# A seven-product down projection whose first and last two steps become eight plain products

## The chip, the cores and the metric

One Trainium2 chip, one NeuronCore. The metric is the device time of one execution in microseconds (us), lower is better. Engines: TensorE (PE in the profile; its weight loads are PEld), VectorE (DVE), ScalarE (ACT), GpSimd (POOL), and SyncE (SP), which here only issues transfers.

## The reference

One inference step of a two-layer trunk: a retention layer, a gated linear attention layer, and behind each a feed-forward network with a causal convolution of width 3. 1024 prompt frames and 32 frames of a running stream (T = 1056 columns), model width 1024, inner width 2816, all float32. The change touches the last feed-forward network's second matrix and the final norm behind it:

```python
def conv_ffn(h, conv_state, w_up, conv_w, conv_b, w_down):
    u = h @ w_up
    ...
    gate, val = jnp.split(c, 2, axis=-1)
    return (jax.nn.silu(gate) * val) @ w_down, ext[:, T:]
...
        y, cs = conv_ffn(h, conv_states[i], ffn_w_up[i], ffn_conv_w[i], ffn_conv_b[i], ffn_w_down[i])
        x = x + y
    return rmsnorm(x, norm_final), ...
```

## The kernel before

**Exactness.** A float32 matrix product is made of three matmuls in the format fp32r: both operands are split into a rounded part ("hi", a cast on ScalarE) and the rest ("lo", a subtraction on VectorE), and hi·hi, hi·lo and lo·hi are added in PSUM.

**Up projection of the last layer** (`ffn_up`, line 1829). 22 tile pairs f of inner width, each by a Winograd form of Strassen's seven products for two halves s of the columns (528 each; the half is cut once more into two quarters of TH = 264, the "b" of the block form). VectorE and ScalarE run the convolution, SiLU and the multiplication (`conv`, line 1858). `pair_sums` (line 1877) then forms, for each pair k of inner tiles (f = 2k, 2k+1; NP = 11 pairs), the seven column combinations that the down projection wants, and stores them to the scratch tensor `scr_h7`, in the order ORD = (1, 2, 6, 5, 7, 4, 3). Pieces 1, 2 and 3 are plain blocks (even tile's first quarter, odd tile's first and second); the others are sums. `ahead_split` (line 1913) splits the pieces of k = 0 and 1, one in each f from 5 to 18, into hi and lo, and stores them to `scr_h2`.

**Down projection** (`Down7`, line 1600). The output has eight tiles of 128 rows, in four pairs p. Step n (0 to 13) handles output pair p = (n+1) mod 4 with a window of at most four K pairs, n-3 to n, cut to 0 to 10; so K pair k is used in steps k to k+3, once for each output pair, and the windows hold 1, 2, 3, then eight times 4, then 3, 2, 1 pairs. For each step, product i of seven and half s, `product` (line 1676) issues three matmuls of 128x264 for each K pair of the window (lines 1689, 1691, 1692). Each half has three PSUM banks a, b and c, where products 1, 6, 7 share a, 2 and 4 share b, 5 and 3 share c; a product that starts a bank anew waits until its previous content is read, and 3, which adds to bank c, waits until line 1707 has read 5 there.

Steps 0 to 9 gather an output block of two quarters in SBUF (`block`: a ring of five blocks for tile 0 of the pair, of three for tile 1), with three ScalarE copies and four VectorE additions for each half (lines 1699 to 1712), and add it to the residual in DRAM by an accumulating transfer (`add`, line 1715, GpSimd's queue); the block returns to its ring when the transfer has landed. Steps 10 to 13 add straight into the residual in SBUF (`settle`, line 1723, after `fetch` has loaded it), square it and, for the last pair, take the final norm and store (`squares`, line 1743; `rms_row` with the matmul of line 231). From step 11 on, the whole of half 0 comes first, then that of half 1.

**What feeds a step.** `weights(k)` (line 1636) asks for a step's two raw matrices (a ring of three raw buffers), splits the first (L1654, L1655), forms sums and differences (L1660 to L1667), and splits those: five casts or copies on ScalarE, eight operations on VectorE, into seven of ten weight buffers. From step 3 on the request stands on GpSimd's queue. `load_x` (line 1618) loads pieces of K pair k on SP's queue; four K pairs live in 28 slots of seven each (slot 7·(k mod 4)+i), so that a piece of pair k+1 goes where that of pair k-3 has just been used. K pairs 0 and 1 come split from `scr_h2`; those from 2 on come raw, and the returned `split` (L1630 on ScalarE, L1633 on VectorE) splits them in place. For k > 3, one is loaded after each product pair of the step before (SP waits for that product), and its split is taken from the list `late` once more than three are there.

**What sets the order.** The kernel is written in program order, but a planner of the framework places each engine's instructions by its own estimate of when they are ready, the place in the program being a priority; `order(a, b)` only forces a behind b. Each engine then works strictly in the placed order, and waits by semaphores. `run` (line 1787) holds the places: weights at i = 0 or 2 of the step before, the last convolution at step 2, `early` (line 1771) the first loads inside the last f of the up projection.

Of the kernel before, what the change touches and what calls it, by code (L numbers as in the profile page):

```python
# [9 lines left out]
F32 = mybir.dt.float32  # L10
# [40 lines left out]
def trunk_kernel(ctx: ExitStack, tc: tile.TileContext, io):  # L51
# [1546 lines left out]
    NP = NF // 2  # L1598

    class Down7:  # L1600

        def __init__(self, sm, regions, AR, HR):
# [3 lines left out]
            self.Y, self.splits, self.ends = {}, [], {}  # L1606
# [11 lines left out]
        def load_x(self, k, i, n=1):  # L1618
            reg, j = self.at[7 * (k % 4) + i]
            v = reg[:, j * 4 * TH:(j + n) * 4 * TH].rearrange("p (m j u) -> p m j u", m=n, j=2)  # L1620
            for m in range(n):
                self.X[k, ORD[i + m]] = v[:, m].rearrange("p j (s t) -> p j s t", s=2)
# [13 lines left out]
        def weights(self, n, home=None, queue=nc.sync):  # L1636
            h = len(self.win[n]) * P
            a, b = slice(0, h), slice(h, 2 * h)
            rg, rv = raw_tile(f"dg{uid()}"), raw_tile(f"dv{uid()}")
            for j, r in enumerate((rg, rv)):  # L1640
                o = self.offs[n] + j * 2 * h * P
                queue.dma_start(r[:, :2 * h], io["w_down7"][o:o + 2 * h * P].rearrange("(p c) -> p c", p=P))

            at = [0]

            def tile(name):
                if home is None:
                    return w_tile(f"{name}{uid()}")
                at[0] += 2 * h
                return home[:, at[0] - 2 * h:at[0]]  # L1650

            def split(src, name):
                hi, lo = tile(name + "h"), tile(name + "l")
                S.copy(hi[:, :2 * h], src[:, :2 * h])  # L1654
                V.tensor_tensor(lo[:, :2 * h], src[:, :2 * h], hi[:, :2 * h].bitcast(F32), op=ALU.subtract)  # L1655
                return [(hi[:, c], lo[:, c]) for c in (a, b)]

            w = self.W[n] = {}
# [4 lines left out]
            v = tile("dwv")  # L1663
# [11 lines left out]

        def product(self, n, s, i):
            m, win = ORD[i], self.win[n]
# [7 lines left out]
            wh, wl = self.W[n][m]  # L1685
            for j, k in enumerate(win):
                c = slice(j * P, j * P + P)
                x = self.X[k, m][:, :, s]
                PE.matmul(ps, wh[:, c], x[:, 0], start=m in (1, 2, 4, 5) and j == 0, stop=False,  # L1689
                          skip_group_check=True)  # L1690
                PE.matmul(ps, wh[:, c], x[:, 1], start=False, stop=False, skip_group_check=True)  # L1691
                mm = PE.matmul(ps, wl[:, c], x[:, 0], start=False, stop=j == len(win) - 1, skip_group_check=True)  # L1692
            self.ends[n, s, i] = mm
# [77 lines left out]
        def early(self, s, i):  # L1771
            if s == 0 and i:
                if i < 4:
                    self.load_x(0, 2 * i - 2, 2)
                elif i == 4:
                    self.load_x(0, 6)
                    self.load_x(1, 0)
                else:
                    self.load_x(1, 2 * i - 9, 2)
                if i == 2:  # L1780
                    self.weights(0)
            if (s, i) == (1, 4):
                self.load_x(1, 5, 2)
            if (s, i) == (1, 5):
                self.weights(1)

        def run(self, last_conv):
# [3 lines left out]
            late, todo = [], []  # L1791
            for n, s, i in seq:
                self.product(n, s, i)
                k = n + 1
                if s == 0:
                    if n < NP - 2 and k > 1 and i == (2 if n > 2 else 0):
                        self.weights(k, None, G if n > 1 else nc.sync)
                    if n == NP - 2 and i == 2:
                        self.weights(k, None, G)
                        self.fetch(3)  # L1800
                    if n == NP - 1 and i in (1, 4):
                        self.weights(NP if i == 1 else NP + 2, None if i == 1 else self.at[21][0][:, 20 * TH:], G)
                    if n == NP - 1 and i in (1, 3, 5):
                        self.fetch(i // 2)
                    if n == NP and i == 0:
                        self.weights(NP + 1, self.at[24][0], G)
                    continue
                if n >= NP:
                    continue
                if n == 2 and i == 1:  # L1810
                    todo = last_conv()
                if todo and n > 2 and i in (2, 5):
                    todo.pop(0)()
                if k in (2, 3):
                    if i == 0:
                        j = 0
                        while j < 7:
                            at = 7 * (k % 4) + j
                            c = 2 if j < 6 and self.at[at][0] is self.at[at + 1][0] else 1
                            self.splits.append(self.load_x(k, j, c))  # L1820
                            j += c
                    elif i > 2:
                        later(self.splits, 2)
                elif 3 < k < NP:
                    late.append(self.load_x(k, i))
                if len(late) > 3 or late and k >= NP:
                    late.pop(0)(self.ends[n, s, i])

    def ffn_up(l, X, fc, sm, he=None, ready=None):
# [47 lines left out]
        def pair_sums(f, c):  # L1877
# [5 lines left out]
            def keep(m, a):  # L1883
                nc.sync.dma_start(io["scr_h7"][k, :, ORD.index(m)], a)
# [8 lines left out]
            if f % 2 == 0:  # L1893
                keep(1, e[:, 0])
                return
# [430 lines left out]
```

## Time and profile before

| | us |
|---|---|
| median of three runs | 2806.88 (2804.42 to 2809.35) |
| profiled execution | 2807.33 |
| its span, first to last instruction | 2805.6 |
| its mean granted clock | 0.996 |
| first matmul of the down projection (L1689), from the span's start | 2542.6 |
| last norm matmul (L231) | 2791.3 |

A row of a list of instructions reads: start, duration, engine, line, operation, output <- inputs, count, and in brackets the idle time before it with what ended it. `pu` is a PSUM bank, `dw..h` and `dw..l` are split weights, `dg` and `dv` the raw ones, XA, XB and XH hold X, AR and HR the blocks and residual. A row of the waits reads: who waited, for whom, us in total, times, the longest. Recorded matmuls overlap: the distance of two starts, not the duration, is the cost of one in a stream.

### The profile page before, as it was taken

To read this page: it belongs to the slowest core of one execution; us is meant where nothing else is said; L and a number is where in the kernel's file an instruction comes from. 1 tells how busy PE (TensorE), PEld (TensorE's weight loads), DVE (VectorE), ACT (ScalarE), POOL (GpSimd) and SP (SyncE) were. 2 spreads that over 40 slices of the span, in tenths; PEclk is the share of its full clock that TensorE was granted. 3 is DMA by queue.
4 is the path that set the end of the run, shared out by engine and by line. 5 is a ranking of instruction groups with operands and counts; after the bars stand their busy time and mean duration, and the time that the engine had idled before them with its cause. 6 is when DMAs were issued, how large, how long until landed. Compare 5 with 4: busy or idle time off the path is not lost.

```text
span 2805.6 us, 54515 instructions
## 1 busy us (share of the span) xinstructions
PE 2757.1 (98%) x21954; PEld 2666.6 (95%) x21954; DVE 1990.9 (71%) x3456; ACT 1353.8 (48%) x2481; POOL 363.3 (13%) x650
## 2 busy tenths in 40 slices
PE   9999999999999999999999999999999999999997
PEld 9999988888999999999999999999999999999996
DVE  7876666676557877777555576775479888888667
ACT  7544354444435444444444466653355444445444
POOL 0000000000112111111000042220132111112222
PEclk9999999999999999999999999999999999999998
DMA  6333455554875222222855501115533434339882
GB/s 239 94 113 100 146 150 150 139 153 121 281 241 183 82 80 82 75 86 73 269 189 163 177 30 53 53 46 200 190 119 100 150 123 154 113 100 292 208 226 91
DMA packets 238974, 395.04 MB, mean 141 GB/s; under 512 B 59008, under 2 KB 162816, under 8 KB 234112
## 3 DMA queue, kind: packets, MB, share of 16 engines
q1 hardware_dynamic: 222960, 333.51, 36.6%
q0 software_dynamic: 15216, 57.50, 7.5%
q8 instruction: 172, 2.82, 0.4%
q14 instruction: 82, 0.67, 0.1%
q10 hardware_dynamic: 544, 0.54, 0.1%
HBM read 272.25 MB, written 119.23 MB: 140 GB/s over the span
## 4 chain that ended last, share of the span: by engine, by line
PE 81%; DVE 7%; ACT 3%; issue 3%; POOL 3%; DMA 2%; SPq 0%; DVEq 0%; POOLq 0%; ACTq 0%
PE pu L441 13%; PE pu L436 13%; PE pu L440 13%; PE pd L1519 5%; PE pd L1521 5%; PE pd L1520 5%; PE psv L270 2%; PE psv L271 2%; PE psv L272 2%; POOL x L1122 2%; PE pu L1689 2%; PE pu L1691 1%; PE pu L1692 1%; PE pg L133 1%; PE pg L134 1%
## 5 line engine op out<-in xcount | busy, mean ns | idle before, releaser
L110 DVE TENSOR_TENSOR wlo<-raw,whi 128x1024 fp32r<-128x1024 f32 x131 | 163.1, 1249 | 126.9 <-ACT whi L110 119.1
L415 ACT COPY HR<-pu 128x264 f32<-128x264 f32 x264 | 98.6, 374 | 264.6 <-PE pu L441 258.6
L110 ACT CAST whi<-raw 128x1024 fp32r<-128x1024 f32 x131 | 136.9, 1049 | 175.5 <-PE pd L1520 111.3
L441 PE MATMUL pu<-XA,wgl 128*128 128x264 f32 x752 | 213.4, 284 | 0.0
L436 PE MATMUL pu<-XA,wgh 128*128 128x264 f32 x752 | 212.9, 283 | 0.0
L440 PE MATMUL pu<-XA,wgh 128*128 128x264 f32 x752 | 212.5, 283 | 0.0
L1866 DVE SCALAR_TENSOR_TENSOR AR<-AR,cw 128x1058 f32<-128x1058 f32 x88 | 115.8, 1318 | 72.8 <-ACT AR L1865 66.9
L1839 DVE TENSOR_TENSOR AR<-HR,pu 128x264 f32<-128x264 f32 (+2 forms) x440 | 144.3, 368 | 5.2 <-PE pu L441 5.1
L1519 PE MATMUL pd<-hh,whi 128*128 128x384 f32 (+1 forms) x440 | 142.2, 323 | 0.0
L1520 PE MATMUL pd<-hl,whi 128*128 128x384 f32 (+1 forms) x440 | 142.2, 323 | 0.1
L1521 PE MATMUL pd<-hh,wlo 128*128 128x384 f32 (+1 forms) x440 | 141.8, 322 | 0.0
L436 PEld LDWEIGHTS pu<-XA,wgh 128*128 128x128 f32 x752 | 141.2, 188 | 0.3 <-ACT wgh L372 0.3
L440 PEld LDWEIGHTS pu<-XA,wgh 128*128 128x128 f32 x752 | 141.2, 188 | 0.0
L441 PEld LDWEIGHTS pu<-XA,wgl 128*128 128x128 f32 x752 | 141.0, 188 | 0.0
L436 PE MATMUL pu<-XA,wsh 128*128 128x264 f32 x464 | 132.5, 286 | 2.5 <-ACT HR L415 1.4
L441 PE MATMUL pu<-XA,wtl 128*128 128x264 f32 x464 | 131.9, 284 | 0.0
L441 PE MATMUL pu<-XA,wsl 128*128 128x264 f32 x464 | 131.8, 284 | 0.0
L436 PE MATMUL pu<-XA,wth 128*128 128x264 f32 x464 | 131.6, 284 | 0.0
L440 PE MATMUL pu<-XA,wsh 128*128 128x264 f32 x464 | 131.3, 283 | 0.0
L440 PE MATMUL pu<-XA,wth 128*128 128x264 f32 x464 | 131.1, 283 | 0.0
L373 DVE TENSOR_TENSOR wtl<-rv,wth 128x1024 fp32r<-128x1024 f32 x58 | 71.0, 1223 | 79.0 <-ACT wth L372 78.9
L1519 PE MATMUL pd<-XH,whi 128*128 128x264 f32 x432 | 123.5, 286 | 0.0
(644 smaller groups left out, 10538.7 us busy)
## 6 DMA issues: line engine op xcount, KB each, us to landing
raw<-w_down SPq DMA_DIRECT2D x60, 512.0 KB, 3.7
rg<-w_up SPq DMA_DIRECT2D x44, 512.0 KB, 3.6
rv<-w_up SPq DMA_DIRECT2D x44, 512.0 KB, 3.5
scr_h<-AR SPq DMA_DIRECT2D x77, 264.0 KB, 2.6
raw<-w_ro SPq DMA_DIRECT2D x39, 512.0 KB, 5.5
XH<-scr_hr POOLq DMA_DIRECT2D x16, 1056.0 KB, 7.1
scr_x<-AR POOLq DMA_DIRECT2D x60, 264.0 KB, 6.5
scr_h<-AR SPq DMA_DIRECT2D x22, 512.0 KB, 2.6
```

Of the source, the lines that this page charges most:

```text
L110: ins = S.copy(hi, raw), V.tensor_tensor(lo, raw, hi.bitcast(F32), op=ALU.subtract)
L270: PE.matmul(ps, ah, hi, start=kt == 0, stop=False)
L373: split_end[0] = split_last[0] = V.tensor_tensor(l_, src, h.bitcast(F32), op=ALU.subtract)
L415: ins = S.copy(t, b)
L436: mm = PE.matmul(ps, wh[:, k], x[:, 0, kt], start=m in (1, 2, 4, 5) and kt == 0, stop=False, skip_group_check=True)
L440: PE.matmul(ps, wh[:, k], x[:, 1, kt], start=False, stop=False, skip_group_check=True)
L441: mm = PE.matmul(ps, wl[:, k], x[:, 0, kt], start=False, stop=kt == 3, skip_group_check=True)
L1519: PE.matmul(o, w[0][:, k], h[0][:, :n], start=i == 0, stop=False)
L1520: PE.matmul(o, w[0][:, k], h[1][:, :n], start=False, stop=False)
L1521: self.last_mm = PE.matmul(o, w[1][:, k], h[0][:, :n], start=False, stop=i == nk - 1)
L1839: last_put[0] = V.tensor_tensor(u[:, d:d + n], t[:, o:o + n], b[:, o:o + n], op=op)
L1866: V.scalar_tensor_tensor(cj, uj[:, 1:T + 3], cw[:, nt, 1:2], cj, op0=ALU.mult, op1=ALU.add)
```

## The change

1. The steps whose window has fewer than three K pairs (0, 1, 12, 13) are made by eight plain products: `plain_product` runs four sums for each half, quarter by quarter (pieces 1 and 2 for the first quarter, 8 and 3 for the second) and tile by tile, each in a PSUM bank of its own, with 2 x 3 matmuls for each K pair. In steps 0 and 1 ScalarE copies each into the block; in 12 and 13 VectorE adds it to the residual.
2. Piece 8 (the even tile's second quarter) is stored for K pairs 0, 1, 9 and 10; the scratch tensors get room for eight pieces. `ahead_split` runs in f from 4 to 19, on 16 pieces. K pairs 9 and 10 load and split theirs in step 11.
3. A plain step's weights are one raw load with one cast and one subtraction, in one or two weight buffers; the host's layout changes with it.
4. Requests for raw weights are parted from their splitting: at i = 0 of the step before (step 2's ahead of the first product), all on SP's queue, none on GpSimd's. Splitting stays at i = 2 (i = 1 for step 2).
5. X copies for k > 3 are taken from the list when more than four are there, one product pair later. Those of k = 2 and 3 are loaded one group at a time, at i = 0 to 3, and split singly.
6. The last convolution is placed at step 4, its sums in step 5. The slots are laid out anew for 28 + 4 pieces.

```diff
+    PIECES = ORD + (8,)
+    EDGE = (0, 1, NP - 2, NP - 1)
...
+            self.plain = [len(w) < 3 for w in self.win]
...
+            homes = [list(range(7)), list(range(8, 15)), list(range(16, 22)) + [15], list(range(22, 28)) + [7]]
+            self.place = {(k, m): homes[k % 4][i] for k in range(NP) for i, m in enumerate(ORD)}
+            self.place.update({(0, 8): 7, (1, 8): 15, (NP - 2, 8): 22, (NP - 1, 8): 23})
...
+        def raw_weights(self, n):
+            h, o = len(self.win[n]) * P, self.offs[n]
+            if self.plain[n]:
+                r = raw_tile(f"dr{uid()}")[:, :4 * h]
+                nc.sync.dma_start(r, io["w_down7"][o:o + 4 * h * P].rearrange("(p c) -> p c", p=P))
+                return r
+            rs = []
+            for j in range(2):
+                r = raw_tile(f"d{'gv'[j]}{uid()}")[:, :2 * h]
+                nc.sync.dma_start(r, io["w_down7"][o + j * 2 * h * P:o + (j + 1) * 2 * h * P].rearrange("(p c) -> p c", p=P))
+                rs.append(r)
+            return rs
...
+            def cut(hi, lo, src):
+                S.copy(hi, src)
+                V.tensor_tensor(lo, src, hi.bitcast(F32), op=ALU.subtract)
+
+            if self.plain[n]:
...
+                cut(hi[:, :4 * h], lo[:, :4 * h], raw)
+                w.update({j: (hi[:, j * h:(j + 1) * h], lo[:, j * h:(j + 1) * h]) for j in range(4)})
+                return
...
+        def terms(self, ps, w, x, first, last):
+            wh, wl = w
+            PE.matmul(ps, wh, x[:, 0], start=first, stop=False, skip_group_check=True)
+            PE.matmul(ps, wh, x[:, 1], start=False, stop=False, skip_group_check=True)
+            return PE.matmul(ps, wl, x[:, 0], start=False, stop=last, skip_group_check=True)
+
+        def plain_product(self, n, s, i):
+            win = self.win[n]
+            half, tile = divmod(i, 2)
+            ps = self.sm("pu")[:, :TH]
+            for j, k in enumerate(win):
+                c = slice(j * P, j * P + P)
+                for h, m in enumerate(((1, 2), (8, 3))[half]):
+                    w = [v[:, c] for v in self.W[n][2 * tile + h]]
+                    self.ends[n, s, i] = self.terms(ps, w, self.X[k, m][:, :, s], j == h == 0,
+                                                    h == 1 and j == len(win) - 1)
+            p, t0 = (n + 1) % 4, 2 * TH * s
+            if n >= NP - 1:
+                y = self.Y[p][:, tile, t0 + half * TH:t0 + half * TH + TH]
+                V.tensor_tensor(y, y, ps, op=ALU.add)
+                if tile:
+                    self.squares(p, s, half)
+                return
+            d = self.unit.setdefault(s, {})
+            if half == 0:
+                d[tile] = self.block(tile)
+            S.copy(d[tile][:, half], ps)
+            if half:
+                self.add(2 * p + tile, t0, d[tile])
...
+            x0 = {1: [(0, 0, 2)], 2: [(0, 2, 2)], 3: [(0, 4, 2)], 4: [(0, 6, 2)], 5: [(1, 0, 2)], 6: [(1, 2, 2)]}
+            x1 = {4: [(1, 4, 2)], 5: [(1, 6, 2)]}
+            for a in (x1 if s else x0).get(i, []):
+                self.load_x(*a)
+            if s == 0 and i == 2:
+                self.weights(0, self.raw_weights(0))
+            if s == 0 and i == 5:
+                self.weights(1, self.raw_weights(1))
...
-                    if n < NP - 2 and k > 1 and i == (2 if n > 2 else 0):
-                        self.weights(k, None, G if n > 1 else nc.sync)
+                    if 2 < k < NP and i == 0:
+                        raws[k] = self.raw_weights(k)
+                    if 1 < k < NP and i == (2 if n > 1 else 1):
+                        self.weights(k, raws.pop(k))
...
-                    if n == NP - 1 and i in (1, 3, 5):
+                    if n == NP - 1 and i in (0, 2, 4):
+                        self.weights(NP + i // 2, self.raw_weights(NP + i // 2))
                         self.fetch(i // 2)
...
+                    if n == NP and i < 2:
+                        splits.append(self.load_x(NP - 2 + i, 7))
+                    if n == NP and 2 < i < 5:
+                        splits.pop(0)(self.ends[n, s, i])
...
-                if n == 2 and i == 1:
+                if n == 4 and i == 1:
                     todo = last_conv()
-                if todo and n > 2 and i in (2, 5):
+                if todo and n > 4 and i in (2, 5):
                     todo.pop(0)()
...
-                if len(late) > 3 or late and k >= NP:
+                if len(late) > 4 or late and k >= NP:
                     late.pop(0)(self.ends[n, s, i])
...
                 keep(1, e[:, 0])
+                if k in EDGE:
+                    keep(8, e[:, 1])
...
-                if he is not None and 4 < f < 19 and (s, i) == (1, 2):
-                    ahead_split(f - 5)
+                if he is not None and 3 < f < 20 and (s, i) == (1, 2):
+                    ahead_split(f - 4)
```

More of the change, by code (lines that the diff above doesn't have):

```diff
@@ L1684, in product @@
             ps = d[bank][:, :TH]
-            wh, wl = self.W[n][m]
             for j, k in enumerate(win):
[L1687 to L1693, printed above, removed]
+                w = [v[:, j * P:j * P + P] for v in self.W[n][m]]
+                self.ends[n, s, i] = self.terms(ps, w, self.X[k, m][:, :, s], m in (1, 2, 4, 5) and j == 0,
+                                                j == len(win) - 1)
             p, t0 = (n + 1) % 4, 2 * TH * s
@@ L1790, in run @@
             seq += [(n, s, i) for s in range(2) for n in range(NP, N) for i in range(7)]
-            late, todo = [], []
+            late, todo, raws, splits = [], [], {2: self.raw_weights(2)}, []
             for n, s, i in seq:
@@ L2224, in _seven_down @@
 def _seven_down(w):
-    w = w.reshape(NF // 2, 2, P, 4, 2, P)
+    n_k = NF // 2
+    w = w.reshape(n_k, 2, P, 4, 2, P)
     out = []
-    for n in range(NF // 2 + 3):
-        k = slice(max(0, n - 3), min(n, NF // 2 - 1) + 1)
-        for j in range(2):
-            out.append(w[k, :, :, (n + 1) % 4, j].transpose(2, 1, 0, 3).ravel())
+    for n in range(n_k + 3):
+        k = slice(max(0, n - 3), min(n, n_k - 1) + 1)
+        v = w[k, :, :, (n + 1) % 4].transpose(3, 2, 1, 0, 4)
+        if v.shape[3] < 3:
+            v = v.transpose(1, 0, 2, 3, 4)
+        out.append(v.ravel())
     return np.concatenate(out)
```

81 lines of the change are left out of this document (30 added, 51 removed).

## The prediction

> **What bounds the kernel now.** I read the page first, then who TensorE waited for in the last fifth of the span, then that stretch by stages.
>
> ```profile
> PE 2757.1 (98%) x21954; PEld 2666.6 (95%) x21954; DVE 1990.9 (71%) x3456; ACT 1353.8 (48%) x2481; POOL 363.3 (13%) x650
> ...
> PE pu L1689 <- DVE AR L1707: 4.6, 4, 2.3
> PE pu L1689 <- DVE AR L1727: 4.2, 4, 1.6
> PE pn L231 <- DVE HR L1754: 2.7, 3, 1.6
> PE pu L1692 <- DVE dwgl L1655: 1.6, 1, 1.6
> PE pu L1689 <- DVE HR L1701: 1.5, 2, 1.0
> PE pu L1691 <- DVE XB L1633: 1.5, 1, 1.5
> ```
>
> The lower six are all the waits of TensorE from 2250 us to the end: together 16.1 us, each on VectorE, and every line but L231 belongs to the seven-product class itself. None falls in the up projection before it, so the two extra look-ahead splits there (16 for 14) and the four new stores of a piece "8" are hidden under TensorE and cost nothing; without that cover they would be some microseconds.
>
> The stretch by stages (columns: stretch, length, busy TensorE, weight load, VectorE, ScalarE, GpSimd with counts, clock, DMA share, GB/s):
>
> ```profile
> 2542.00:2548.00 6.00, 5.99 (x47) 5.61 (x46) 4.75 (x9) 5.03 (x10) 1.43 (x2) 1.00 1.02 411
> 2548.00:2561.00 13.00, 10.39 (x80) 9.85 (x80) 12.19 (x21) 9.98 (x16) 4.13 (x5) 1.00 1.07 319
> 2578.00:2600.00 22.00, 20.51 (x167) 20.11 (x165) 17.86 (x29) 8.71 (x15) 5.16 (x7) 1.00 0.98 275
> 2621.00:2642.00 21.00, 21.00 (x175) 21.00 (x174) 14.39 (x25) 10.24 (x18) 4.96 (x8) 1.00 0.83 201
> 2746.00:2762.00 16.00, 14.41 (x117) 14.10 (x116) 10.94 (x24) 9.46 (x22) 6.31 (x9) 1.00 0.00 0
> 2773.00:2790.00 17.00, 15.64 (x122) 15.00 (x121) 15.21 (x34) 7.22 (x19) 6.27 (x7) 0.98 0.38 128
> ```
>
> In an undisturbed step (2621 to 2642) 175 matmuls take 21.00 us: one is worth 0.120 us, though its record lasts 0.28. VectorE is nearly full in steps 0 and 1 (12.19 of 13) and at the very end (15.21 of 17), and has a third free in a full step. So the edges are bound by VectorE, the middle by TensorE.
>
> The waits in the middle are not VectorE's amount of work. The chain of waits, the waits of all engines, and two rows of ScalarE:
>
> ```profile
> 2567.58 4.20 DMA dv<-w_down
> 2593.19 5.88 DMA dv<-w_down
> 2674.59 7.91 DMA XA<-scr_h
> 2715.75 7.69 DMA XA<-scr_h
> ...
> DVE dv L1660 <- DMA dv<-w_down: 35.7, 11, 6.7
> ...
> 2682.52 0.63 ACT L1630 CAST XA<-XA 128x528 fp32r<-128x528 f32 x1 [4.47 <-DMA XA<-scr_h]
> 2722.31 0.63 ACT L1630 CAST XA<-XA 128x528 fp32r<-128x528 f32 x1 [5.16 <-DMA XA<-scr_h]
> ```
>
> VectorE stands 35.7 us on the weights' second half (asked for on GpSimd's queue), and ScalarE 4.47 and 5.16 us on a late X piece; the L1707 evictions queue behind both, and four matmuls wait for those:
>
> ```profile
> 2564.37 0.39 PE L1689 MATMUL pu<-XA,dwsh 128*128 128x264 f32 x1 [0.60 <-DVE AR L1707]
> 2601.39 0.39 PE L1689 MATMUL pu<-XA,dwsh 128*128 128x264 f32 x1 [1.36 <-DVE AR L1707]
> 2685.76 0.39 PE L1689 MATMUL pu<-XA,dwsh 128*128 128x264 f32 x1 [2.27 <-DVE AR L1707]
> 2727.29 0.39 PE L1689 MATMUL pu<-XB,dwsh 128*128 128x264 f32 x1 [0.36 <-DVE AR L1707]
> ```
>
> **The change, part by part.** *More matmuls.* Steps 0 and 13 hold one K pair, 1 and 12 two; eight products for seven add 3 matmuls for each K pair and token half: (1+2+2+1) x 3 x 2 = 36, at 0.120: **+4.3 us**, with nothing to hide it.
>
> *Steps 0 and 1* waited 1.6 (dwgl, L1655) and 1.0 us (L1701). Their VectorE work, from these rows:
>
> ```profile
> 2544.49 0.42 DVE L1701 TENSOR_TENSOR HR<-HR,pu 128x264 f32<-128x264 f32 x1
> 2550.26 0.69 DVE L1655 TENSOR_TENSOR dwgl<-dg,dwgh 128x512 fp32r<-128x512 f32 x1
> 2550.86 0.42 DVE L1660 TENSOR_TENSOR dv<-dv 128x256 f32<-128x256 f32 x1
> 2576.71 1.22 DVE L1655 TENSOR_TENSOR dwsl<-dg,dwsh 128x1024 fp32r<-128x1024 f32 x1
> 2543.20 0.38 ACT L1699 COPY HR<-pu 128x264 f32<-128x264 f32 x1 [0.19 <-PE pu L1692]
> ```
>
> Four evictions for each half and step go (16 x 0.42 = 6.7), and step 1's eight weight operations (3 x 0.69 + 5 x 0.42 = 4.2) become one of 1.22. That is some 10 us less of 17. ScalarE gets one copy more for each half and step, 4 x 0.38 = 1.5 us, and three weight casts fewer. Both waits go: **-2.6**. Bounds: none goes, or both.
>
> *Steps 1 to 3* waited 0.5 (L1701's other), 1.5 (L1633), 0.60 and 1.36 us: 4.0. The weights are asked for two product pairs ahead on SP's queue, when both raw buffers are free, so the 35.7 us on VectorE should largely vanish; the last convolution moves from step 2 to 4. That move is worth little: its place is only a priority, as this row shows, part of that convolution run in step 0.
>
> ```profile
> 2543.26 1.31 DVE L1866 SCALAR_TENSOR_TENSOR AR<-AR,cw 128x1058 f32<-128x1058 f32 x1
> ```
>
> I keep 0.6 of the 4.0: **-3.4**; bounds 0 and -4.0. On SP the raw requests stand among the X loads, each of which waits for a product; the accumulating transfers alone stay on GpSimd's.
>
> *X copies one product pair later* (24 matmuls, 2.9 us): 4.47 and 5.16 us of ScalarE waiting shrink to 1.6 and 2.3, and the 2.27 and 0.36 us of TensorE behind them vanish: **-2.6**; bounds 0 and -2.6. What comes closer is a piece's own use, now two product pairs, 5.8 us, after its copy; copy and subtraction take 0.63 and 0.71.
>
> ```profile
> 2683.19 0.71 DVE L1633 TENSOR_TENSOR XA<-XA 128x528 fp32r<-128x528 f32 x1 [4.55 <-ACT XA L1630]
> ```
>
> *Steps 12 and 13.* The first half's end and its norm waited 1.59 and 1.48 (these rows) plus 1.1 on L231, 4.2 in all; the second half's steps the remaining 1.1 of L1727.
>
> ```profile
> 2753.22 0.39 PE L1689 MATMUL pu<-XA,dwsh 128*128 128x264 f32 x1 [1.59 <-DVE AR L1727]
> 2768.19 0.39 PE L1689 MATMUL pu<-XB 128*128 128x264 f32 x1 [1.48 <-DVE AR L1727]
> ```
>
> Each of these steps has four evictions for a half in place of seven, and two weight operations in place of twelve. A norm's matmul still waits for squares, so I keep 1.5 of the 4.2: **-2.7**, and take all of the other: **-1.1**; bounds 0 and -5.3 together. The two extra piece loads (K pairs 9 and 10) come where the DMA share is 0.00 (2746 to 2762), with two copies and subtractions: nothing; late, they would hold step 12.
>
> *After the last matmul* 16 us remain. From here VectorE works for both quarters one behind the other:
>
> ```profile
> 2791.32 1.91 PE L231 MATMUL pn<-HR,ones 128*128 128x264 f32 x3 [1.55 <-DVE HR L1754]
> 2792.61 0.48 ACT L243 ACTIVATE rt<-pn,epsc 128x264 f32<-128x264 f32 x1 [1.18 <-PE pn L231]
> 2800.64 0.48 DVE L1767 SCALAR_TENSOR_TENSOR AR<-AR,gcol,R 128x264 f32<-128x264 f32 x1
> ```
>
> The first quarter is now complete two products of six matmuls (1.4 us) before the last, not one of three (0.4), so this chain starts 1.0 earlier, and the 1.55 shrinks: **-1.5**; bounds 0 and -3.
>
> *A new wait.* All plain evictions go through ScalarE into blocks returned only when their accumulation has landed. Tile 1 has a ring of three. Step 0 fills the first by 5.4 us (7 of 8 products of 6 matmuls, and a copy); an accumulation takes:
>
> ```profile
> 2548.46 1.86 POOL L1716 DMA_DIRECT2D scr_x<-AR  x2 [3.72 <-DVE AR L1709]
> ...
> DMA to landing us min/median/max: 4.1/6.8/10.2
> ```
>
> So it returns after 12.2 to 15.6 us; the fourth is wanted in step 1 after 5.8 + 4 x 1.44 = 11.5. ScalarE stands 0.7 to 4.1 us, with weight casts and X copies for step 2 behind it. TensorE runs on into free PSUM banks: price 0 to 4.1; I take **+1.5**, nearer the lower since the banks cover it first.
>
> The sum: 4.3 - 2.6 - 3.4 - 2.6 - 2.7 - 1.1 - 1.5 + 1.5 = -8.1. The profiled run took 2807.33 us (span 2805.6, 1.7 around it), so **2799.2**; its own time stands 0.4 above the median of 2806.88, which is nothing.
>
> **The rivals.** *The waits only move*: VectorE's order, not its load, makes them, and the block wait takes 4.1. Then only 2.6, 1.1 and half of the middle's 6.6 go: 4.3 + 4.1 - 7.0 = +1.4, 2808.7; with the tail's 1.5, 2807. For it: steps 1 to 3 wait with VectorE at 17.86 of 22, so load alone isn't the cause. Against: the named cause, the late weights, is what the change moves.
>
> *Slower: SP's one queue makes X late.* These rows are the transfers of the stretch:
>
> ```profile
> XA<-scr_h SPq DMA_DIRECT2D x32, 264.0 KB, 5.1
> ...
> dg<-w_down POOLq DMA_DIRECT2D x8, 512.0 KB, 5.2
> ```
>
> Up to 1 MB of weights now goes ahead of a step's first X pieces on the same queue. A copy follows its load by four pairs, 11.5 us; 5.2 + 5.1 = 10.3 fits, 5.2 + 7.9 (the chain's slow X piece) doesn't. If each of seven steps (3 to 9) repeated the 2.27 us, that is +15.9, and -8.1 becomes +7.8: 2815. It decides from about 0.8 us a step, where the gain is gone. Against: those waits occurred in two steps only, with a margin 2.9 us smaller.
>
> [...]
>
> **How the numbers follow.** From no change a measurement tells 0.2%, 5.6 us. Forecast 0.66; the waits move 0.19; slower by the queue 0.11, and by late copies or a block wait that reaches step 2 in full with the middle's gain lost 0.04. Faster 0.67, same 0.18, slower 0.15. All waits gone with the tail's 3 is 4.3 - 14.5 - 3 = -13.2, and each of 14 matmuls after a wait is recorded at 0.39, not 0.28 (1.5 more): 2792. Above, the second rival with a margin: 2812, leaving out most of the third.
>
> **What would show it.** Right: about 1884 matmuls (1848 before) in the plain and seven-product lines together; no dwgl and L1701 wait before 2560; VectorE's wait for the weights under 10 us; no L1707 wait over 1 us after step 3; last matmul to end under 15 us. Wrong: ScalarE waiting on accumulations in step 1 for over 4 us; X waits above 4 us in more than two steps; or TensorE's waits in this stretch above 12 us.

## The result, and the profile after

The changed kernel took 2813.2 us (median, 2811.89 to 2815.84) beside 2805.88 us for the kernel before: ratio 1.0026, 95% interval 1.0015 to 1.0037. It is slower by 7 us, with an interval that lies above 1, where 8 us less was forecast. Its profiled execution took 2811.89 us with a span of 2810.1, 4.6 above that of before; the rest of the 7 lies in where the two profiled executions stand among their runs. From the first matmul of the down projection to the end of the span (the stretch, below) it was 267.5 us (2542.6 to 2810.1) in place of 263.0 (2542.6 to 2805.6), so the loss is there.

The page's first line, then all waits of TensorE in the stretch (microseconds in all, times, longest):

```profile
PE 2760.4 (98%) x21990; PEld 2671.1 (95%) x21990; DVE 1975.9 (70%) x3404; ACT 1355.2 (48%) x2477; POOL 352.5 (13%) x628
```

```profile
PE pn L231 <- DVE HR L1807: 12.0, 4, 4.5
PE pu L1702 <- ACT HR L1756: 2.8, 1, 2.8
PE pu L1702 <- DVE AR L1760: 1.4, 3, 0.8
PE pu L1702 <- ACT AR L1752: 1.0, 1, 1.0
PE pu L1703 <- DVE XB L1642: 0.6, 1, 0.6
PE pu L1702 <- DVE AR L1780: 0.4, 1, 0.4
PE pu L1702 <- ACT AR L1756: 0.4, 1, 0.4
```

VectorE does 15 us less (1975.9 for 1990.9), and still TensorE waits 18.6 us in place of 16.1. The waits changed hands: the norm's matmul (L231) went from 2.7 to 12.0, and three rows wait for ScalarE, which none did before. By stages (2542 to 2561 is steps 0 and 1, 2561 to 2583 step 2 and the start of 3), after and then before:

```profile
2542.00:2561.00 19.00, 19.00 (x158) 18.97 (x156) 13.13 (x18) 11.66 (x21) 4.98 (x6) 1.00 1.04 341
2561.00:2583.00 22.00, 17.23 (x121) 16.24 (x120) 17.97 (x24) 14.60 (x23) 3.57 (x5) 0.92 0.99 300
```

```profile
2542.00:2561.00 19.00, 16.38 (x126) 15.46 (x125) 16.93 (x29) 15.01 (x25) 5.56 (x7) 1.00 1.05 348
2561.00:2583.00 22.00, 19.41 (x153) 18.61 (x152) 19.10 (x32) 11.54 (x20) 5.69 (x8) 1.00 0.89 224
```

Steps 0 and 1 run without a gap, 2.6 us better. The next 22 us give 2.2 of that back, at a granted clock of 0.92 where it had been 1.00. There ScalarE stands in front of transfers (waits for transfers of VectorE and ScalarE; then two rows of ScalarE and the matmul behind them):

```profile
DVE dv L1684 <- DMA dv<-w_down: 33.1, 9, 7.0
ACT AR L1726 <- DMA scr_x<-AR: 3.2, 1, 3.2
ACT XH L1639 <- DMA XH<-scr_h: 3.0, 2, 2.9
```

```profile
2574.40 1.07 ACT L1639 CAST XH<-XH 128x1056 fp32r<-128x1056 f32 x1 [2.87 <-DMA XH<-scr_h]
2575.38 0.37 ACT L1756 COPY HR<-pu 128x264 f32<-128x264 f32 x1
2575.80 0.39 PE L1702 MATMUL pu<-XA,dwth 128*128 128x264 f32 x1 [2.85 <-ACT HR L1756]
```

The eviction at 2575.38 stands in ScalarE's order behind the copy of an X piece of K pair 3 (loaded for step 3), whose transfer is late; TensorE needs the eviction's PSUM bank. At the end of a token half (here the second) it is VectorE's order:

```profile
2793.11 0.71 PE L231 MATMUL pn<-HR,ones 128*128 128x264 f32 x2 [1.50 <-DVE HR L1807]
...
2795.02 0.28 PE L1704 MATMUL pu<-XA,dp 128*128 128x264 f32 x1
...
2796.10 0.42 ACT L1806 ACTIVATE HR<-AR 128x264 f32<-128x264 f32 x1 [0.43 <-DVE AR L1719]
...
2796.67 1.94 DVE L1816 TENSOR_TENSOR AR<-AR,R 128x528 f32<-128x528 f32 x3
...
2798.53 0.89 DVE L1820 SCALAR_TENSOR_TENSOR AR<-AR,gcol,R 128x264 f32<-128x264 f32 x2
2799.33 0.42 DVE L1807 TENSOR_TENSOR HR<-HR 128x264 f32<-128x264 f32 x1
...
2799.81 0.81 PE L231 MATMUL pn<-HR,ones 128*128 128x264 f32 x1 [4.51 <-DVE HR L1807]
```

The second quarter's last square is ready at 2796.5, but its sum (L1807) runs at 2799.33, behind the first quarter's whole scaling (L1816, L1820). With plain products the first quarter is complete two products before the second instead of one, so its norm is issued between them (its matmul at 2793.11 stands ahead of the last product, whose last matmul is that of 2795.02). The first half does the same at 2766.76 and 2773.47 (1.50 and 4.52), and there half 1's first products wait behind it.

### The profile page after: what moved, and what is told of

The parts are those of the page before. It is cut to its first block, busy times and chain, and to the rows that moved or that the text cites. A ratio compares the mean times of both kernels' runs of the same rounds, so it can differ in the third digit from the quotient of the medians.

```text
span 2810.1 us, 54549 instructions
## 1 busy us (share of the span) xinstructions
PE 2760.4 (98%) x21990; PEld 2671.1 (95%) x21990; DVE 1975.9 (70%) x3404; ACT 1355.2 (48%) x2477; POOL 352.5 (13%) x628
## 4 chain that ended last, share of the span: by engine, by line
PE 79%; DVE 7%; issue 5%; ACT 3%; POOL 3%; DMA 2%; SPq 0%; DVEq 0%; POOLq 0%; ACTq 0%
PE pu L441 13%; PE pu L436 13%; PE pu L440 13%; PE pd L1519 5%; PE pd L1521 5%; PE pd L1520 5%; PE psv L270 2%; PE psv L271 2%; PE psv L272 2%; POOL x L1122 2%; DMA raw<-w_ro 1%; PE pg L133 1%; PE pg L134 1%; PE pg L135 1%; PE pu L1702 1%
## 5 line engine op out<-in xcount | busy, mean ns | idle before, releaser
L1521 PE MATMUL pd<-XH,wlo 128*128 128x264 f32 x432 | 122.4, 284 | 0.2 <-DVE wlo L110 0.2
```

The costliest lines, as they stand in the source:

```text
L1521: self.last_mm = PE.matmul(o, w[1][:, k], h[0][:, :n], start=False, stop=i == nk - 1)
```

## The experiments

All were timed in five rounds beside the kernel before; ratios are to before, with the 95% interval. "Stretch" is that of one profiled execution, so a difference of 2 us in it may be chance (the twelve executions of e1 alone took 2800.19 to 2812.33 us). In the diffs A marks an edit of the changed kernel, B one of the kernel before.

### Which half of the change loses

**a1: plain products in steps 0 and 1 alone** (A). In it step 12's weights are written into slots from which K pair 7 is still read, so what is computed there differs from the reference; c2 is the same split with the weights elsewhere.

```diff
-            self.plain = [len(w) < 3 for w in self.win]
+            self.plain = [n < 2 for n in range(NP + 3)]
```

> The change with plain products in steps 0 and 1 only; steps 12 and 13 stay seven products, their weights in free slots as before the change. Theory A (the last steps' order costs: the first quarter's norm stands ahead of the second quarter's sums on VectorE, two waits of 4.5 us at the norm's matmul): 2.2 us more matmuls and the waits of steps 0 to 3 little changed, so 2805 to 2808, norm waits back to 3 us in all. Rival B (the first steps cost: all their evictions on ScalarE, which waits for a block): 2811 or more.

**a2: plain products in steps 12 and 13 alone** (A). The eighth pieces of K pairs 0 and 1 are neither stored nor loaded, and step 1's weights are asked for where the kernel before asked, in the last f's second token half in place of its first; the rest is the change's.

```diff
-            self.plain = [len(w) < 3 for w in self.win]
+            self.plain = [n > NP for n in range(NP + 3)]
```

> The change with plain products in steps 12 and 13 only; steps 0 and 1 are seven products. Theory A: the norm waits of 12 us stay, so 2810 to 2814. Rival B: 2808 or less.

**c2: as a1, step 12's weights asked for one step later, in step 11, when those slots are free** (A).

> Plain products in steps 0 and 1 only, once more, with step 12's weights written at the start of step 11 as before the change, and all outputs as the reference's. Rival B now (the first steps alone lose): about 2810, with 2.2 us of matmuls, and waits of 4 to 5 us in steps 1 to 3 as large as those of before. If the first steps gain what the prediction said, it is 2803 to 2806.

Measured: a1 1.0033 (1.0021 to 1.0046), c2 1.0029 (1.0018 to 1.0040), a2 1.0013 (1.0004 to 1.0022). Each half loses alone. But the first two can't price steps 0 and 1: the seven products of their last steps, with weights placed and asked for in another way, wait too. In c2:

```profile
PE pu L1709 <- DVE AR L1787: 6.5, 6, 2.1
PE pu L1709 <- ACT AR L1763: 4.6, 1, 4.6
```

L1787 is what L1727 was before (4.2 there); the second row is step 2. a2 keeps the changed kernel's row L231, 12.0 in 4.

### The norms at the end of a half

**a4: both quarters' norms behind both quarters' sums** (A).

```diff
-            rms_row([ss], t0, n, self.sm("pn"), None, False)
+            self.norms.append((ss, t0, n, s, half))
+            if half:
+                self.finish()
```

> The change with both quarters' norms placed behind both quarters' sums of squares in step 13, for each half. Theory A: the two waits of 4.5 us fall to about 1 each and the 1.5 us ones vanish, so 6 to 9 us less than the change: 2804 to 2807. Rival B: the norm's order is hidden anyway, 2812 or more.

Ratio 1.0001 (0.9992 to 1.0010): 7 us back, all that the change had lost. A half's two waits became one:

```profile
PE pn L231 <- DVE HR L1808: 4.4, 2, 3.8
```

**c1: only the scaling and the stores of the first quarter behind the second's norm** (A).

```diff
+            self.norms.append((t0, n, s, half))
+            if half:
+                for a in self.norms:
+                    self.store(*a)
```

> The change with one thing moved: the five VectorE operations that scale the first quarter by its norm, and their stores, stand behind the second quarter's norm; each norm's matmul keeps its place. Theory A: the 4.5 us waits fall to 1 to 2.5 us each, the 1.5 us ones stay; 3 to 6 us less than the change, 2808 to 2811 where before is 2806. Rival (it is the norm matmul's place on TensorE, not the queue on VectorE): the 4.5 us waits stay, 2813.

Ratio 1.0008 (0.9997 to 1.0019), an interval that still meets the change's. Its second norm (row of the second half):

```profile
2798.87 0.71 PE L231 MATMUL pn<-HR,ones 128*128 128x264 f32 x2 [2.47 <-DVE HR L1808]
```

4.51 became 2.47: the scaling ahead of the sum was 2.0 us of each half. The 2.5 left stand while the first norm's chain (L243 to L250) runs on the same two engines, with one of the scalings (0.70 us at 2797.77) still ahead of the last sum; the first norm's 1.5 stayed.

**b4 and c3: half 0's norms behind the third product of half 1's step 11** (A); in b4 half 1's stand behind both sums, in c3 where the change has them.

```diff
+                if (n, i) == (NP, 2):
+                    self.finish()
```

> The change with both norms of half 0 placed behind the third product of half 1's step 11, and those of half 1 behind both quarters' sums. Theory A: half 0's norm waits vanish altogether; against the change 8 to 10 us less, 2803 to 2805, and 1 to 2 less than with the norms only behind the sums. Rival: PSUM banks or VectorE's load in half 1 give it back, 2807.

> The change with half 0's norms behind the third product of half 1's step 11, half 1's as in the change. Theory A: of the 7.6 us that TensorE loses at half 0's norms nearly all goes, half 1's 4.5 stays: 6 to 7 us less than the change, 2806 to 2807 where before is 2806. Rival: the norm's work lands on VectorE in steps 11 and 12 of half 1 and delays their additions, 2810.

b4: 1.0006 (0.9996 to 1.0015), no better than a4. c3: 1.0011 (1.0001 to 1.0022); half 0's waits are gone, but half 1's, alone now, grew:

```profile
2789.88 1.25 PE L231 MATMUL pn<-HR,ones 128*128 128x264 f32 x2 [6.01 <-DVE HR L1808]
...
2797.83 1.25 PE L231 MATMUL pn<-HR,ones 128*128 128x264 f32 x2 [4.07 <-DVE HR L1808]
```

**d4: plain products in steps 12 and 13 alone, norms as in a4** (A).

> Plain products in steps 12 and 13 alone, with both norms of a half behind both its sums. Theory that the first steps cost the changed kernel about as much as they give and the norms' place is all of the last steps' loss: the wait on L231 falls from 12 us to about 4.5, the stretch from 268.4 to 263 to 265, ratio to before 0.999 to 1.001. Rival that plain products at the end lose for another reason too (18 more matmuls, their sums on VectorE): ratio above 1.0015, stretch 266 or more.

Ratio 0.9987 (0.9979 to 0.9996), stretch 262.6: the only version whose interval lies below 1, by 3.6 us; the two medians (2806.21 and 2806.91) are only 0.7 apart. With a2, a4 and the change it makes a square:

```
                         norms as in the change   norms behind both sums
plain in all four steps          1.0026                 1.0001
plain in the last two            1.0013                 0.9987
```

Along each row the norms' place is worth 7.0 and 7.3 us, with intervals that don't overlap. Down each column plain first steps, with their extra loads and the earlier request of step 1's weights, cost 3.6 and 3.9; there the intervals overlap. Within this noise the two add up. d4's step 2 has no wait on an eviction like that of 2575.38 (TensorE's longest on ScalarE in the stretch is 1.0 us), so e1's edit has nothing to mend there; the two were not run together.

### What plain first steps cost

**b1: the fourth tile-1 block from the other ring** (A).

```diff
-                d[tile] = self.block(tile)
+                d[tile] = self.block(0 if (n, s) == (1, 1) else tile)
```

> The change with the fourth tile-1 block of steps 0 and 1 taken from the other ring, which has a free fifth, so that no copy waits for an accumulation there. Theory (the block wait of 3.2 us on ScalarE delays steps 1 and 2): TensorE's waits of step 2 (0.6, 1.0, 0.4 and 2.8 us) shrink by 2 or more, 2810 to 2812. Rival (the late X pieces of K pair 3 make these waits): ScalarE's wait for the block goes, TensorE's stay, 2813.

Ratio 1.0051 (1.0036 to 1.0067), stretch 273.3. ScalarE's wait for the block in step 1 is gone and step 2's waits stay; but the ring is now shifted by one for all later steps, and the first square's buffer, which shares HR with the blocks, is still held by an accumulation:

```profile
PE pu L1702 <- DVE AR L1780: 4.7, 2, 4.3
PE pu L1702 <- ACT HR L1756: 4.0, 2, 2.6
...
ACT HR L1802 <- DMA scr_x<-HR: 11.7, 1, 11.7
```

**d2: evictions of plain products by VectorE** (A).

```diff
-            S.copy(d[tile][:, half], ps)
+            V.tensor_copy(d[tile][:, half], ps)
```

> The changed kernel with the evictions of the plain products of steps 0 and 1 on VectorE in place of ScalarE (the wait for a tile-1 block then stands on VectorE). Theory: the 3.2 us that ScalarE stands for the block at 2559 delays its copies of step 2's X and weights and so TensorE's waits in 2560 to 2576; with the evictions on VectorE ScalarE has no block wait and TensorE's waits in step 2 fall by 2 us or more from 5. Rival: the transfers set those copies (2.9 on XH, 2.0 on the weights), the waits of step 2 stay within 1 us of 5, and the time stays within 0.05% of the changed kernel's.

Ratio 1.0022 (1.0013 to 1.0031), as the change. ScalarE has no block wait, and comes to the same late transfers earlier:

```profile
PE pu L1702 <- ACT HR L1756: 3.4, 1, 3.4
PE pu L1703 <- DVE XB L1642: 1.9, 1, 1.9
...
ACT XB L1639 <- DMA XB<-scr_h: 6.2, 3, 3.3
ACT XH L1639 <- DMA XH<-scr_h: 3.7, 2, 3.2
```

So the block wait, the prediction's +1.5, was not what TensorE paid for: it waits 4.8 us in step 2 in the change, 5.0 in b1, which has no such wait, and 5.3 in d2.

**b2: K pairs 2 and 3 asked for and copied as before** (A).

```diff
-                    if i < 4:
-                        splits.append(self.load_x(k, *groups[i]))
+                    if i == 0:
+                        splits.extend(self.load_x(k, *g) for g in ((0, 2), (2, 2), (4, 2)))
```

> The change with the loads of K pairs 2 and 3 asked for together at i = 0 and split two at a time from i = 3, as before the change (one piece of pair 2 keeps its place, where piece 8 stood). Theory (X copies of pair 3 stand too early on ScalarE, before their transfers have landed): the 2.8 us wait behind an XH transfer goes, 2809 to 2811. Rival: the transfers are late whatever asks for them, and the wait moves to another copy, 2813.

Ratio 1.0026 (1.0016 to 1.0035); step 2 waits 2.9 us on the same eviction.

**d3: no plain product, but the eighth pieces' loads** (A; step 1's weights are asked for where the kernel before asked).

```diff
-            self.plain = [len(w) < 3 for w in self.win]
+            self.plain = [False] * (NP + 3)
```

> No plain product at all: all fourteen steps by seven products, but with the eight stored pieces of K pairs 0 and 1, their loads, the early request of the raw weights and the later copies as in the changed kernel. Theory that the plain products' faster first steps bring step 2 forward onto transfers that come when they come: without them no wait for XH and no fall of the granted clock in 2570 to 2590, and the down stretch is 262 to 265 as before. Rival that the added bytes of the eighth pieces make the transfers late: step 2 waits 3 us or more on ScalarE, the granted clock falls below 0.95 there, the stretch is 266 or more.

Ratio 1.0022 (1.0014 to 1.0031), stretch 269.5. Step 1's weights, asked for behind the two more pieces, are late:

```profile
2554.66 0.59 PE L1709 MATMUL pu<-XA,dwgh 128*128 128x264 f32 x1 [5.01 <-ACT dwgh L1671]
```

The last steps are c2's here (L1787 again 6.5), so only this row counts: with seven products the added loads hurt in step 1. b3 (below), with the early requests and without these loads, has no such row (its one wait for weights is 1.6 us); nor has the change, which asks for step 1's weights earlier. Step 2 has no wait for XH here and a clock of 1.00, as the theory said; the stretch is long for the other two reasons.

**e2: the change with a4's norms and without the eighth pieces' loads** (A; the plain products of steps 0 and 1 read piece 3 in place of 8).

```diff
-            x1 = {4: [(1, 4, 2)], 5: [(1, 6, 2)]}
+            x1 = {4: [(1, 4, 2)], 5: [(1, 6, 1)]}
```

> The changed kernel with both norms of a half behind both its sums, and without the two loads of the eighth pieces of K pairs 0 and 1 (two times 528 KB); the plain products of steps 0 and 1 take piece 3 where they would take piece 8, so that part is not computed as in the reference. Theory that bytes in a stretch where the transfers are the limit make step 2's transfers late: ScalarE's waits for XH, XA and the weights in step 2 fall from 7 us to below 3, TensorE's waits in step 2 from 5 to below 2.5, the stretch to 261 to 263.5. Rival: the transfers of step 2 are late by where they are asked, the waits stay within 1 us, the stretch stays 264.5 to 266.

Ratio 1.0003 (0.9995 to 1.0012), stretch 264.3. The bytes are not what makes step 2 wait in the change:

```profile
PE pu L1703 <- ACT AR L1758: 3.2, 1, 3.2
PE pu L1703 <- ACT AR L1754: 1.8, 1, 1.8
...
ACT XH L1640 <- DMA XH<-scr_h: 4.2, 1, 4.2
```

**d1 and e1: K pair 3's copies later in step 2, with a4's norms** (A). d1 moved the calls alone; the order on ScalarE is the planner's, and came out as in a4, so d1 tells nothing of the place and is a second measure of a4. e1 holds each copy behind a product's last matmul:

```diff
-                        later(splits, 1)
+                        for _ in range(min(1 if i < 6 else 2, len(splits))):
+                            splits.pop(0)(self.ends[n, s, i])
```

> The changed kernel with both norms of a half behind both its quarters' sums, and with ScalarE's copies of K pair 3's X moved from behind products 2 to 5 of step 2 to behind products 4 to 6. Theory: in step 2 ScalarE stands 2.9 us in front of the copy of XH, whose transfer is late, and the eviction of a product stands behind that copy, so TensorE waits 2.9 us and the clock granted next to it falls. Then TensorE's wait on the HR eviction falls below 1 us, the granted clock in 2570 to 2590 is 1.00, and the down stretch is 3 to 4.5 us shorter than with the norms moved alone (265.3), 261 to 262.5. Rival: the transfers are late by more than the two products, so the same wait comes at the same place or at the first products of step 3, and the stretch stays within 1 us of 265.3.

> The changed kernel with both norms of a half behind both its sums, and with K pair 3's copies held behind the matmuls of products 4 to 6 of step 2 by an ordering, so that ScalarE's order itself changes: the evictions of those products stand ahead of the copies of XH. Theory: TensorE's 2.4 us wait on the HR eviction in step 2 (ScalarE in front of a late XH) goes below 1 us, the granted clock stays 1.00 in 2570 to 2590, and the stretch is 262 to 264 in place of 265.3. Rival: the waits move to the weights' copies or to the first products of step 3, and the stretch stays 265 to 267.

d1: 1.0005 (0.9996 to 1.0013). e1: 0.9995 (0.9985 to 1.0005). The window from 2561 to 2583, first of a4 and then of e1, and e1's evictions ahead of the copies:

```profile
2561.00:2583.00 22.00, 17.14 (x121) 16.29 (x122) 17.65 (x24) 13.96 (x22) 3.25 (x5) 0.92 0.97 296
```

```profile
2561.00:2583.00 22.00, 20.13 (x160) 19.40 (x159) 19.51 (x29) 13.19 (x22) 4.29 (x5) 1.00 1.07 314
```

```profile
2568.46 0.37 ACT L1757 COPY AR<-pu 128x264 f32<-128x264 f32 x1
2568.73 0.38 ACT L1757 COPY HR<-pu 128x264 f32<-128x264 f32 x1
...
2574.13 1.09 ACT L1640 CAST XH<-XH 128x1056 fp32r<-128x1056 f32 x1
```

TensorE's wait on the HR eviction is gone, ScalarE's for XH too, the clock is 1.00, and 39 more matmuls are recorded in the window. The transfer need not come sooner: the copy of it must not stand ahead of an eviction. In time this is worth 1.7 to 2.8 us against a4 and d1, with intervals that overlap, so the trace shows this cause and the times alone would not. e1's stretch of 258.8 flatters it: its profiled execution (2800.91 us) is 3.8 below its median of 2804.7, and a4's and d1's longest wait on L1761, which stands behind step 2, where e1 changes nothing, is 2.5 and 2.2 us beside e1's 1.3. In 2730 to 2740 d1's granted clock is 0.83 beside e1's 1.00.

### The two edits of the middle, alone

**a3: the kernel before with X copies one product pair later** (B), **b3: with the raw weights asked for early on SP's queue** (B), **c4: a3 with half 0's norms in half 1's step 11** (B).

```diff
-                if len(late) > 3 or late and k >= NP:
+                if len(late) > 4 or late and k >= NP:
```

```diff
+                    if 2 < k < NP and i == 0:
+                        raws[k] = self.raw_weights(k)
+                    if 1 < k < NP and i == (2 if n > 1 else 1):
+                        self.weights(k, None, raws.pop(k))
```

> The kernel before with X copies one product pair later and nothing else. If that edit is worth what the prediction's term says, TensorE's waits of 2.27 and 0.36 us go and the time is 2803 to 2804. Rival: VectorE then waits as long on the late weights, and the time stays within 1 us of before.

> The kernel before with the raw weights asked for as in the change (SP's queue, two product pairs ahead) and nothing else. The prediction's term: VectorE's wait for the weights (35.7 us) falls below 10 and TensorE's waits of steps 1 to 3 by 3: 3 us less than before. Rival: the third raw buffer, not the queue, makes the second half late, so VectorE's wait stays above 25 us and the time within 1 us.

> The kernel before, seven products everywhere, with two edits: X copies one pair later, and half 0's norms behind the third product of half 1's step 11. If the matmuls of the plain steps are the price and the order of the norm the rest, this is the best of both: 2.6 and 3 to 4 us less than before, 2799 to 2802 where before is 2806. Rival: what stalls the middle moves on, 2804.

a3 0.9998 (0.9989 to 1.0007), b3 1.0002 (0.9993 to 1.0011), c4 0.9999 (0.9988 to 1.0009): none can be told from before. The intervals of b3 and c4 exclude the gains foreseen (3 us, and 5.6 to 6.6); a3's, 3.1 us down to 2.0 up, leaves room for its 2.6. In a3 the L1707 waits fell from 4.6 to 1.9 and ScalarE's longest wait for an X piece from 5.16 to 2.0, as foreseen; in b3 VectorE's wait for the weights stayed above 25 us, as the rival said. The rows, first a3's and then b3's:

```profile
PE pu L1689 <- DVE AR L1707: 1.9, 2, 1.3
...
ACT XA L1630 <- DMA XA<-scr_h: 3.5, 2, 2.0
```

```profile
DVE dv L1667 <- DMA dv<-w_down: 32.9, 9, 5.9
```

## Why the prediction failed

Its terms against the profiled execution, TensorE's waits from the rows above and the windows:

```
term                              forecast   after against before
36 more matmuls                     +4.3     +4.3 (x21990 for x21954, at 0.120)
steps 0 and 1                       -2.6     -2.6 (no wait before 2561)
steps 1 to 3                        -3.4     +0.8 (2.8 + 1.0 + 0.6 + 0.4 for 4.0)
X copies later                      -2.6     -1.2 (L1760's 1.4 for 2.63)
first half's end and norm           -2.7     +2.2 (0.4 + 1.50 + 4.52 for 4.2)
second half's end                   -1.1     +0.4 (1.50 for 1.1)
last matmul to end                  -1.5     -1.0 (2810.1 - 2795.3 = 14.8 for 15.8)
clock in 2561 to 2583                 -      +1.8 (22 x 0.08)
block wait                          +1.5     in "steps 1 to 3"
sum                                 -8.1     +4.7 (the stretch: +4.5)
```

That the sum fits to 0.2 is partly luck: falls of the clock beside the first half's norms are left out (0.66 in 2770 to 2775 before; 0.68 and 0.63 in the two windows of 5 us from 2770 after), and they would add up to 1.8.

**Right:** the matmuls; steps 0 and 1, in size and reason; the later X copies in mechanism (for K pairs from 4 on ScalarE no longer waits above 1 us on them, and the 2.27 is gone), half the size forecast, since step 9 keeps 0.36 and gets 0.84 for another reason (below), and not to be told from nothing alone (a3). ScalarE's block wait was 3.2, inside its 0.7 to 4.1; b1 and d2 show that TensorE didn't pay for it. The weights of a full step are four casts or copies on ScalarE, not the five told above the prediction; with VectorE's eight they make the twelve that the prediction counts. One of its signs of being wrong came: TensorE's waits above 12 us, at 18.6.

**The first step that failed** is "steps 12 and 13": "each of these steps has four evictions for a half in place of seven", so the waits shrink. The work did shrink; the order was not followed. The same sentence that took 1.5 us off the tail, that the first quarter is complete two products earlier, puts that quarter's norm and scaling ahead of the second quarter's sum on an engine that works in the placed order (the sum at 2799.33, its square ready at 2796.5). The first half was never costed for it, and a wait there isn't a tail but holds half 1's first matmuls. a4 and c1 show it: 7 us by the norms' place, 2.0 of each 4.5 by the scaling. No rival named it.

**The second** is "steps 1 to 3": the weights asked for earlier, "when both raw buffers are free", so that "the 35.7 us on VectorE should largely vanish". It is 33.1, and b3's is 32.9. Only one buffer is free then. The ring has three, so the second half of a step's weights (`dv`) takes the buffer that holds the first half (`dg`) of the step before, and its request stands until VectorE has read that for the last time, in the subtraction of `dws`. VectorE's next operation on weights wants the new half, so it waits for a landing, whatever queue asks (GpSimd's before, SP's in the change and in b3); in the changed kernel:

```profile
2610.67 1.22 DVE L1665 TENSOR_TENSOR dwsl<-dg,dwsh 128x1024 fp32r<-128x1024 f32 x1
2611.92 0.33 SPq L1654 DMA_DIRECT2D dv<-w_down  x1
2615.95 0.69 DVE L1684 TENSOR_TENSOR dv<-dv 128x512 f32<-128x512 f32 x1 [3.18 <-DMA dv<-w_down]
```

Before, the same request left GpSimd at 2611.61, after a subtraction that ended at 2611.25. No run has a fourth buffer, so what one would give is not shown. Of the 33.1 us TensorE's rows show little: in step 9 VectorE's longest such wait (6.99 us, to 2724.13) holds an eviction, and TensorE waits 0.84 us at 2725.08 (a4's longest wait on this eviction is 2.5). In the kernel before, the 1.36 us of step 3 stood behind such a wait too (3.30 us, to 2599.17).

What TensorE waits for in step 2 of the change is ScalarE's order (e1), neither the block (b1, d2), nor where X is asked for (b2), nor the eighth pieces' bytes (e2). The prediction counted ScalarE's added copies as work (1.5 us) and gave no price to the order of its copies and evictions with a late transfer at its head. Why that transfer keeps ScalarE 2.87 us in the change and 1.6 before stays open.

**The rivals:** the queue rival ended on the right side by a mechanism that did not occur: X waits of 4 us or more never came back in steps 3 to 9 (in the whole stretch ScalarE waits 0.2 us on XA and 0.2 on XB), so its +15.9 was not there. b3, with the weights on SP's queue and X copies as before, has ScalarE wait 5.2 us on XA in place of 9.9, so these weights did not make X late. (The 0.8 us a step at which the prediction saw the gain gone leaves 2.5 of it; it is gone at 1.2.) "The waits only move" was nearest, VectorE's order and not its load, but it was priced at +1.4 and had the tail for a gain.

## What to carry to other kernels

When two pieces of work on an engine that keeps its placed order are completed further apart, look at what the first releases into the gap: a chain that is short on the page can stand ahead of the second's last small operation (4.5 us of wait at each half's second norm, 2.0 of them by the scaling), and it cost more where the next stage's matmuls queue behind it (+2.2 us at the first half's end, +0.4 at the second's). When evictions and copies of loaded data share an engine, a copy belongs behind the evictions that are due before its transfer lands, and the order has to be read from the trace, not from the program (e1: a wait of TensorE of 2.35 us in a4 and 2.68 in d1 is gone). An engine's wait in the list (VectorE's 35 us) is worth only what the bound engine loses behind it, to be read from that engine's rows. And before a request is moved to an earlier place, look at which buffer it fills and who reads that last.

## What the runs showed of the hardware

In several traces the granted clock fell beside a wait of TensorE, so time was lost beyond the wait itself. In the changed kernel two waits, 0.35 and 2.85 us, stood close together, and the granted clock fell (windows of 5 us):

```profile
2570.00:2575.00 5.00, 2.60 (x20) 2.17 (x18) 1.92 (x4) 1.50 (x3) 0.00 (x0) 1.00 1.07 326
2575.00:2580.00 5.00, 4.20 (x24) 4.20 (x25) 4.50 (x5) 4.85 (x8) 0.00 (x0) 0.73 0.97 319
2580.00:2585.00 5.00, 5.00 (x39) 4.83 (x38) 4.50 (x9) 1.77 (x4) 2.17 (x3) 0.93 0.73 202
```

5 x 0.27 and 5 x 0.07 make 1.7 us lost, an estimate from the clock of these windows (in the last, TensorE is busy throughout and 39 matmuls take 5.00 us, 0.128 each for 0.120); a4 shows 0.83 in one window of 10, the same 1.7, and e1, without the wait, none. It does not always: in b2 TensorE waits 0.45 and 2.87 us at the same two places, and the clock stays at 1.00 (the second of these rows; the changed kernel's has 0.98):

```profile
2577.08 0.39 PE L1702 MATMUL pu<-XA,dwth 128*128 128x264 f32 x1 [2.87 <-ACT HR L1756]
2544.01:2615.00 70.99, 64.82 (x524) 63.76 (x522) 51.72 (x74) 38.33 (x66) 15.31 (x18) 1.00 0.97 278
```

In e2 TensorE waits 1.77 us, until 2564.80, and 3.19, until 2574.29: the clock is 0.83 in 2560 to 2570, and 1.00 in 2570 to 2580, with the longer wait, and in the ten us behind. So the 1.7 us belong to some executions with this wait, its length alone does not decide, and what does isn't shown.
